# A set order of TensorE, VectorE and ScalarE while the weights of a matrix product come in

## The chip, the cores and the metric

One core of one Trainium2 chip runs the kernel. The metric is device time in microseconds (us), the median of several executions. The profile is of one execution, so its span (1517.6 us before) differs by a few us from the medians.

## The reference, cut to what matters

```python
B, S, D = 8, 2048, 2048            # x: B x S x D, w: D x D, float32
cs = np.cumsum(x, axis=1)
diff = cs - np.concatenate([zeros, cs[:, :-1, :]], axis=1)   # x again
return np.matmul(diff, w).astype(np.float32)
```

The running sum and its difference cancel, so the work is x @ w: 128 row tiles of x (128 x 2048 each) times a 2048 x 2048 matrix.

## The kernel before: the parts that matter

In the long run the kernel scales w to 16 bit (one scale for all of w) and multiplies tiles of x in groups of four with a Strassen-like scheme, which needs sums and differences of blocks of w. It cannot begin that before all of w has come in, because the scale needs the maximum of all of w. So while w arrives (32 pieces of 512 KB), TensorE multiplies the first three row tiles plainly in bf16, with each piece cast by ScalarE and its absolute maximum taken by VectorE. The x of these three tiles is cast, turned on TensorE (a transpose into PSUM) and copied out. A fourth tile ("late") is turned the same way and multiplied with the scaled w. The program is written in a framework that orders instructions by itself where nothing is said; `tc.issue_after` fixes an order.

```python
def turn(t, xf, i):
    v = bank(6 + i % 2).bitcast(bf16)[:, :NB]
    xb = ring.tile([P, NB], bf16, name="xb", bufs=3)
    nc.vector.tensor_copy(xb, xf)                       # cast of x
    for kk in range(KQ):
        at = ds(kk * P, P)
        nc.tensor.transpose(v[:, at], xb[:, at], eye)
    ...  # copy v to t, on ScalarE or VectorE by turns

def taken(h, ko):                                       # one piece of w
    ...
    nc.scalar.copy(b, wt)                               # cast to bf16
    nc.vector.tensor_reduce(wmax[:, i : i + 1], wt, AX.X, MAX, apply_absolute_value=True)

for h in range(2):                                      # left, right half of w
    for ko in range(KO - KQ):
        if h == 0 and ko == KQ:
            for q in range(1, 4):
                load_x(q)
        fetch(h, ko)
        if h == 0 and ko == 0:
            turn_x(0)
        if h == 0 and KQ <= ko < KQ + 3:
            turn_x(ko - KQ + 1)
        taken(h, ko)
        for r in range(EARLY):
            plain(h, r, ko)                             # two products
    ...  # the last four pieces; for h == 1 the late tile's turns and the maximum of all
    for r in range(EARLY):
        for ko in range(KO - KQ, KO):
            plain(h, r, ko)
        plain_out(h, r)                                 # PSUM to SBUF, ScalarE or VectorE
```

Then come three tiles of the first group. Each is loaded, measured, narrowed to 16 bit, and transposed by DMA.

```python
def prepare(t, waste, xf=None):
    ...  # load of x on SyncE's queue
    m, _ = measure(xf, waste)      # ScalarE; writes a result nobody reads into "waste"
    s, _ = invert(m)
    xh, _ = narrow(xf, s)
    xT = place(t)
    turn_over(xT, xh)              # DMA transposition, on SyncE's queue
    return m, xT

got[PLAIN] = prepare(PLAIN, waste)
...  # scaling of w, 32 instructions on VectorE and ScalarE
got[PLAIN + 1] = prepare(PLAIN + 1, waste, ...)
got[PLAIN + 2] = prepare(PLAIN + 2, waste)
...
put(c, rows, ds(h * NH + n * NB, NB))      # the late tile's stores, GpSimd
...
fetch_x(PLAIN + 3)                         # loads of the next tiles, SyncE
fetch_x(PLAIN + 4)
```

## Time and profile before

| | before |
|---|---|
| median of the three runs that the prediction knew (with the fourth: 1520.87) | 1521.25 us (1518.13 to 1521.31) |
| profiled span | 1517.6 us |
| TensorE busy in the profile | 98% |
| VectorE, ScalarE busy | 73%, 57% |
| 6840 products at 0.2159 us | 1476.8 us |

A busy share averages over stages. A product's recorded duration (379 ns) overlaps the next one's, so "busy" hides slow spacing; count the products instead.

### The profile page before, as it was taken

Reading aid. Unit: us, or ns where it says so; the run is one execution under the profiler, and the core shown is the slowest. Engines: PE = TensorE matmul, PEld = TensorE weight load, DVE = VectorE, ACT = ScalarE, POOL = GpSimd, SP = SyncE. Lnnn points to the kernel's source line nnn. Section 1 sums busy time; section 2 is a strip of 40 time slices with the busy share of each in tenths; the row PEclk is TensorE's granted clock in tenths of the full one; section 3 lists DMA queues with packets and bytes.
Section 4 is the critical chain, followed back from the end, with each engine's and each line's share of the span. In section 5 each row is a group of like instructions: output and inputs, shape, how many; then the busy total and the mean of one; then the engine's idle time right before and its main releaser. Section 6 shows DMA issues by size and latency. Waiting matters only on the chain. (4 is left out here: it accounts for less than half of the span.)

```text
span 1517.6 us, 19099 instructions
## 1 busy us (share of the span) xinstructions
PE 1493.7 (98%) x6904; PEld 674.1 (44%) x6904; DVE 1105.5 (73%) x2067; ACT 861.9 (57%) x1102; POOL 9.8 (1%) x21
## 2 busy tenths in 40 slices
PE   7999999999999999999999999999999999999998
PEld 3344444444444444444444444444444444444443
DVE  7896876767776766776767776767776767777767
ACT  5866555656555656555665555565556565556551
POOL 0100000000000000000000000000000000000000
PEclk9999999999999999999999999999999999999999
DMA  9978788778878788788788788788877887887772
GB/s 363 359 192 222 226 246 218 237 219 240 221 240 219 232 225 247 217 243 223 221 236 239 218 240 230 214 223 247 232 236 208 231 230 233 241 233 222 220 207 111
DMA packets 321470, 351.49 MB, mean 232 GB/s; under 512 B 266848, under 2 KB 266848, under 8 KB 305376
## 3 DMA queue, kind: packets, MB, share of 16 engines
q1 hardware_dynamic: 319808, 345.56, 79.0%
q0 software_dynamic: 1280, 4.20, 0.8%
q8 instruction: 54, 0.88, 0.2%
q10 hardware_dynamic: 288, 0.52, 0.1%
q14 instruction: 40, 0.33, 0.1%
HBM read 150.99 MB, written 134.22 MB: 188 GB/s over the span
## 5 line engine op out<-in xcount | busy, mean ns | idle before, releaser
L414 DVE SCALAR_TENSOR_TENSOR c<-b,u,c 128x512 f32<-128x512 f32 (+1 forms) x883 | 674.9, 799 | 232.2 <-ACT c L409 110.3
L409 ACT ACTIVATE c<-b,u 128x512 f32<-128x512 f32 x496 | 315.1, 680 | 279.6 <-PE b L367 184.7
L367 PE MATMUL b<-W,xT 128*128 128x512 f16 x2048 | 462.5, 379 | 1.7 <-DVE c L414 1.1
L367 PE MATMUL b<-W,W 128*128 128x512 f16 x1764 | 412.1, 379 | 1.4 <-ACT c L409 1.4
L105 ACT ACTIVATE c<-fin 128x2048 f16<-128x2048 f32 x92 | 175.7, 1910 | 243.9 <-DMA out_dram<-c 216.6
L367 PEld LDWEIGHTS <-xT 128*128 128x128 f16 x2048 | 200.3, 98 | 243.9 <-issue 2.7
L367 PEld LDWEIGHTS <-W 128*128 128x128 f16 x2016 | 197.2, 98 | 239.8 <-issue 2.3
L116 ACT ACTIVATE fin<-fin,s 128x2048 f16<-128x2048 f32 x123 | 246.2, 2002 | 88.3 <-issue 45.2
L378 PEld LDWEIGHTS <-W 128*128 128x128 f16 x1560 | 152.2, 98 | 187.0 <-issue 2.4
L378 PE MATMUL b<-W,W 128*128 128x512 f16 x810 | 220.0, 379 | 0.8 <-DVE c L414 0.7
L378 PE MATMUL b<-W,xT 128*128 128x512 f16 x720 | 179.9, 379 | 0.0
L378 PE MATMUL b<-inner,W 128*128 128x512 f16 x660 | 176.4, 379 | 0.0
L378 PEld LDWEIGHTS <-xT 128*128 128x128 f16 x960 | 93.9, 98 | 113.3
L473 DVE TENSOR_REDUCE m<-m 128x1 f32<-128x4 f32 x29 | 4.6, 157 | 106.9 <-ACT b L465 106.9
L465 ACT ACTIVATE b<-fin 128x512 f32<-128x512 f32 x116 | 68.0, 586 | 13.7 <-DMA fin<-in_x_dram 13.4
L367 PE MATMUL b<-W 128*128 128x512 f16 x252 | 75.1, 379 | 0.1
L423 DVE TENSOR_TENSOR W<-W,xT 128x1024 f16<-128x1024 f16 x122 | 68.2, 559 | 3.2
L423 DVE TENSOR_TENSOR W<-xT,W 128x1024 f16<-128x1024 f16 x122 | 67.4, 552 | 0.0
L378 PE MATMUL b<-inner,xT 128*128 128x512 f16 x240 | 61.6, 379 | 0.0
L423 DVE TENSOR_TENSOR W<-xT,xT 128x1024 f16<-128x1024 f16 (+1 forms) x92 | 54.8, 596 | 1.1 <-DMA xT<-fin 1.1
L111 DVE TENSOR_SCALAR m<-m 128x1 f32<-128x1 f32 x124 | 18.5, 149 | 42.9 <-ACT c L105 41.6
L212 PE MATMUL b<-wb,xP 128*128 128x512 bf16 x192 | 46.5, 406 | 2.7 <-ACT wb L204 2.7
(56 smaller groups left out, 471.9 us busy)
## 6 DMA issues: line engine op xcount, KB each, us to landing
fin<-in_x_dram SPq DMA_DIRECT2D x124, 1024.0 KB, 5.5
out_dram<-c SPq DMA_DIRECT2D x247, 512.0 KB, 3.2
W<-in_w_dram SPq DMA_DIRECT2D x32, 512.0 KB, 10.2
W<-in_x_dram SPq DMA_DIRECT2D x12, 256.0 KB, 6.5
xT<-fin SPq DMA_TRANSPOSE x184, 5.0
out_dram<-o POOLq DMA_DIRECT2D x10, 256.0 KB, 5.2
out_dram<-wb POOLq DMA_DIRECT2D x6, 256.0 KB, 9.7
xP<-in_x_dram SPq DMA_DIRECT2D x1, 1024.0 KB, 7.4
```

Source lines behind the costliest of these rows:

```text
L105: return m, nc.scalar.activation(waste.bitcast(f16), xf, ABS, scale=1.0 / ROW, accum_out=m)
L111: nc.vector.tensor_scalar(m, m, TINY, None, MAX)
L116: return xh, nc.scalar.activation(xh, xf, COPY, scale=s)
L212: nc.tensor.matmul(ps[r][n], xP[:, r, ko, :], wb[h, ko][:, ds(n * NB, NB)], start=(ko == 0), stop=(ko == KO - 1),)
L367: nc.tensor.matmul(ps[n], a[k], b[k][:, n, :], start=(first and k == 0), stop=(k == KH - 1), skip_group_check=True,)
L378: nc.tensor.matmul(ps, a[k], b[k], start=(first and k == 0), stop=(k == 3), skip_group_check=True)
L409: after("act", lambda: nc.scalar.activation(c, p, COPY, scale=scale))
L414: "dve", lambda: nc.vector.scalar_tensor_tensor(c, p, scale, c, MUL, ADD)
L423: after("dve", lambda: nc.vector.tensor_tensor(dst.all, p.all, q.all, op))
L465: lambda: nc.scalar.activation(ps[i % 2], xf[:, at], ABS, scale=1.0 / ROW, accum_out=m4[:, i : i + 1],),
L473: after("dve", lambda: nc.vector.tensor_reduce(m, m4, AX.X, ADD))
```

## The change

Its intent is that TensorE always finds its next operand. All instructions of TensorE, VectorE and ScalarE in the w stage are chained in the order in which they are written; the x of the plain tiles is loaded a quarter at a time between pieces of w; its casts stand ahead of that step's maximum and its turns between the products of a step; three casts of the right half stand ahead of the left half's copies; the late tile's turns stand behind the last products. In the first group, the load of a tile goes behind two stores and the measurement's waste goes to another buffer.

```diff
-        def turn(t, xf, i):
+        def cast(xf):
+            xb = ring.tile([P, NB], bf16, name="xb", bufs=3)
+            after("dve", lambda: nc.vector.tensor_copy(xb, xf))
+            return xb
+
+        def turn(t, xb, i):
             v = bank(6 + i % 2).bitcast(bf16)[:, :NB]
-            xb = ring.tile([P, NB], bf16, name="xb", bufs=3)
-            nc.vector.tensor_copy(xb, xf)
             for kk in range(KQ):
                 at = ds(kk * P, P)
-                nc.tensor.transpose(v[:, at], xb[:, at], eye)
+                after("pe", lambda: nc.tensor.transpose(v[:, at], xb[:, at], eye))
 ...  (the same wrapping for the casts of w, maxima, products and copies out)
+        AHEAD = 3
+        LOOK = KQ - 1, KQ + 1, KQ + 3
 ...
+                if h == 0:
+                    if KQ - 1 <= ko < KQ + 2:
+                        load_x(ko - KQ + 2)
+                    fetch(h, ko)
+                    if ko == 0:
+                        for r in range(EARLY):
+                            turn_x(0, r, cast(resting(0, r)))
+                    if ko in LOOK:
+                        q = LOOK.index(ko) + 1
+                        xb = [cast(resting(q, r)) for r in range(EARLY)]
+                    taken(h, ko)
+                elif ko >= AHEAD:
+                    fetch(h, ko)
+                    taken(h, ko)
                 for r in range(EARLY):
                     plain(h, r, ko)
+                    if xb:
+                        turn_x(q, r, xb[r])
 ...
+            if h == 0:
+                for ko in range(AHEAD):
+                    fetch(1, ko)
+                for ko in range(AHEAD):
+                    taken(1, ko)
 ...  (first group)
         turn(g + 4)
-        fetch_x(g + 5)
 ...
         put(C12g, g, 1)
+        fetch_x(g + 5)
 ...
-        weigh(g + 5, b)
+        weigh(g + 5, c)
```

## The prediction

> **What bounds the kernel now.** I first read the busy time of each engine by stage, cutting the span where the timeline of TensorE changes character. Columns: stretch in us, its length, busy us (and instructions) of TensorE, of its weight loads, of VectorE (DVE), ScalarE (ACT) and GpSimd, the granted clock, the DMA share, GB/s.
>
> ```profile
> 0.00:23.00 23.00, 12.91 (x72) 6.58 (x73) 14.39 (x30) 9.80 (x13) 0.19 (x4) 0.94 0.91 334
> 23.00:41.40 18.40, 17.70 (x72) 7.50 (x72) 15.23 (x16) 12.59 (x15) 0.00 (x0) 0.89 1.03 409
> 41.40:63.00 21.60, 21.12 (x96) 9.27 (x95) 18.80 (x21) 16.59 (x21) 4.06 (x8) 1.00 0.91 362
> 63.00:84.40 21.40, 18.00 (x80) 7.18 (x81) 20.99 (x42) 21.40 (x22) 3.45 (x7) 1.00 0.97 291
> 84.40:134.00 49.60, 46.47 (x212) 20.59 (x211) 36.52 (x77) 25.49 (x29) 2.15 (x4) 1.00 0.71 190
> 134.00:400.00 266.00, 265.80 (x1232) 120.15 (x1230) 197.49 (x387) 152.26 (x200) 0.00 (x0) 1.00 0.84 232
> 400.00:800.00 400.00, 400.00 (x1853) 181.06 (x1852) 287.44 (x543) 229.58 (x299) 0.00 (x0) 1.00 0.81 229
> ```
>
> From 400 to 800 us, 1853 matmuls take 400 us: 0.2159 us each, no gap. From 134 us on TensorE is the whole bound (1232 x 0.2159 = 266.0 in 266.0). Before that, 256 products and 64 transposes take 84.4 us where 256 x 0.2159 = 55.3 would do, 29 us lost; 212 products take 49.6 instead of 45.8, 3.8 lost. The last 318 us lose 6.5 more (1443 x 0.2159 = 311.5) at the tail. The diff touches no part of the steady groups or the tail, so at most about 33 us are in play, and less because w has to arrive.
>
> Who sets the end of the first 84 us? I followed VectorE through it (start, us, engine, line, operation, count, [idle before <- releaser]).
>
> ```profile
> 22.25 14.73 DVE L206 TENSOR_REDUCE wmax<-W 128x1 f32<-128x1024 f32 x13
> 40.16 1.29 DVE L233 COPY o<-b 128x512 f32<-128x512 f32 x2 [3.17 <-PE b L212]
> 41.36 16.98 DVE L206 TENSOR_REDUCE wmax<-W 128x1 f32<-128x1024 f32 x15
> 58.38 0.19 DVE L263 TENSOR_REDUCE wred<-wmax 128x1 f32<-128x32 f32 x1
> ...
> 59.52 0.75 DVE L282 TENSOR_SCALAR W<-W,uinv 128x1024 f16<-128x1024 f32 x1
> 62.40 0.69 DVE L233 COPY wb<-b 128x512 f32<-128x512 f32 x1 [2.13 <-PE b L212]
> ```
>
> The maxima of w (1.13 us each, 32 of them) run back to back to 58.38, although DMA ran out of queued work at about 57.5 and the last w came some microseconds sooner (2 MB of x, 5 us at 410 GB/s, were queued behind it). Only after the last maximum does the scale exist, and only then can the 25 scalings of w on VectorE (0.67 each) and the seven on ScalarE (1.1 each) start. They end at 82.55 and 83.53; the late tile's 64 products trickle behind them and end at 84.57. So in this stretch the bound is VectorE's queue, then ScalarE's; TensorE, which has only 13.8 us of work after 63, is not. Any TensorE time saved ahead of 63 us counts only so far as it releases VectorE or ScalarE.
>
> The 3.8 us after 84.4 are plain waits in TensorE's timeline:
>
> ```profile
> 128.16 0.38 PE L367 MATMUL b<-W,W 128*128 128x512 f16 x1 [1.17 <-ACT c L409]
> ...
> 133.00 0.38 PE L367 MATMUL b<-W,xT 128*128 128x512 f16 x1 [0.87 <-DVE c L414]
> ```
>
> with 0.20 and 0.28 beside them and 0.56 at 102.43. ScalarE itself stood still for 4.30 us until 127.42 on a store (out_dram<-c), then 1.21 more on another store before it could measure a tile. In the DMA queue of SyncE, the load of x at 118.99 had waited for its buffer, and three stores whose data was older sat behind it, issued only from 119.37.
>
> ```profile
> 127.42 1.26 ACT L409 ACTIVATE c<-b,u 128x512 f32<-128x512 f32 x2 [4.30 <-DMA out_dram<-c]
> 129.89 1.91 ACT L105 ACTIVATE c<-fin 128x2048 f16<-128x2048 f32 x1 [1.21 <-DMA out_dram<-c]
> ...
> 118.99 0.34 SPq L99 DMA_DIRECT2D fin<-in_x_dram  x1
> 119.37 1.86 SPq L419 DMA_DIRECT2D out_dram<-c  x3
> ```
>
> **What the Trainium skill says.** "TensorE: Matmul & The Clock Gate", section "Architectural detail: the array is 16× 32×32, not 1× 128×128", says ScalarE and VectorE take their queues strictly in order and TensorE runs its matmuls in order. The trace agrees: VectorE idled 3.17 us ahead of two copies although more w was there for the maxima behind them. So where an instruction stands is what the change really changes. The same page, "What's actually happening", says the array falls to half clock when it has been idle: the granted clock was 0.50 from 22 to 26 us, after the transposes, and the products there were issued 0.43 us apart. "Perfetto Trace Analysis", section "Roofline", puts 16 DMA engines at about 435 GB/s for one core; 409 GB/s at a full DMA share from 23 to 41 us is near that, so w cannot come faster.
>
> **The change, part by part.** It adds and removes no data work: the built program has 13810 rows on TensorE in both. It moves instructions.
>
> 1. Turns of x between products (loads of x spread over w3 to w5, casts ahead of that step's maximum). Saved: TensorE's stretch from 16.36 to 23.07, 6.7 us of transposes alone, and the half clock after it (72 products in 17.70, 2.15 over 72 x 0.2159). Paid: each turn now waits for its own w block and comes between ScalarE's casts. I scheduled it by hand with the trace's arrivals (w3 at 14.5 instead of 12.2, w5 20.9, w7 23.5) and durations (cast of w 1.04, maximum 1.13, product 0.216, four transposes about 0.5 to their end, copy 0.4). TensorE begins the steps 3, 5, 7 and 8 at about 15.6, 22.0, 27.2 and 30.5. In the kernel before it has done 25 of its 72 products by 30.5 (10 at half clock, then full), thus also stands at step 8. So the left half ends at about 30.5 + 48 x 0.2159 = 40.9 against 40.8: no gain, the idle time is only cut into pieces.
>
> 2. VectorE in that stretch. Before, its idle time between 4.1 and 58.4 is 1.10 + 0.70 + 0.85 + 0.44 + 1.71 + 0.16 + 0.49 + 0.80 + 3.17 = 9.4 us. After, the 3.17 goes (row by row order of the last 24 products frees banks 3.5 us before the end, and two maxima are put ahead of the copies), but in the three turning steps the copies out of PSUM stand right behind a maximum and wait for a product and the transposes: 0.85 + 1.0, 1.6, 0.7 + 1.0 = 5.2 us in place of about 3.2. With waits for w0 to w3 (about 2 us) and the first two (1.8) I get 9 to 9.5 us. The last maximum therefore stands where it was, 58.4, give or take 1.5.
>
> 3. Three right-half casts ahead of the stores: TensorE's 1.03 us wait at 41.79 for a cast goes. But VectorE reaches its two copies with 11 maxima still to do from 29.95: 29.95 + 11 x 1.13 = 42.4, done 43.7, so the right half's first step may wait 2 us for these banks and TensorE may end at 63.9 instead of 62.9. Off the path, as shown above.
>
> 4. After the scale. In the built order three scalings now stand before VectorE's first copy instead of one, so they fill the 2.13 us it idled; ScalarE's first copies need only the first row's products (at about 60.4, not 61.9, since the order of the last 24 stays row by row). VectorE's last scaling: 59.6 + 25 x 0.67 + copies 1.3 + casts 1.45 + late copies 0.75 + small ones 0.9 = 80.7, plus about 0.6 of waiting, 81.3 against 82.55. ScalarE from 60.4 instead of 61.9 over 21.6 us of work ends at about 82.1 against 83.53. The late stage so ends at about 83.2 instead of 84.5: **1.3 us gained**.
>
> 5. First group: the load of x goes behind the stores of C22 and C12, and the measurement's waste goes to buffer c. The store of C22 can be issued at about 115.3, after the transposes in the queue, instead of 119.4, so ScalarE's copy no longer waits until 127.4 and the 1.37 us at 128 go; the measurement does not wait 1.21, and the 1.15 at 133 go with it. The load itself waited for its buffer until 118.99 anyway and loses little. **2.5 us gained.**
>
> Sum 3.8 us; 1521.25 - 3.8 = 1517.4, put at 1517.3.
>
> **Rivals.** (a) Interleaving really lifts the w stage: if VectorE's copies find the transposes ready, its idle falls from 9.4 to about 5 us and the scale comes 4 us earlier: 1513. For it: the intent, and 44 us of VectorE work in a 54 us stage. Against: its strict order behind w's arrivals. (b) The interleaved turns leave TensorE under-fed from 16 to 30 us (about 30 products and 36 transposes, some 60% busy), the clock falls to half for longer and drags the copies and the maxima: 2 to 4 us given back, 1519 to 1521. For it: the 0.50 at 22 to 26 us. (c) x of the first group arrives late because its load is now behind stores, so that the stall at 128 is merely replaced by one on the measurement: the 2.5 us vanish, 1520. Against: the load waited for a buffer, not for its place.
>
> **Range and chances.** The late end is uncertain by about 2.5 us, the stall by 1, and three runs of before alone spread 3 us. Together some 3 to 4 us either way, with rival (a) stretching the fast side: 1511.5 to 1521. Two per cent is 30 us, all that is lost before 134 us with w not yet there for most of it: faster 0.01, slower 0.005, the rest within.
>
> **What would show it.** Right: last maximum within 57 to 60 us, the scalings' end at 81 to 82.5 on both engines, first product of the group at 83 to 84, no wait over 0.3 us from 125 to 134, the stretch from 134 on unchanged. Wrong: the last maximum before 56 (rival a), a granted clock of 0.50 for over 6 us (b), a wait on a measurement near 128 (c), or any new wait in the steady groups.

## The result

The changed kernel took 1521.17 us (median of four runs, 1519.15 to 1522.44), the kernel before 1520.87 in the same rounds. A ratio here is the mean time of one kernel's runs over that of the other's of the same rounds, so it is not quite the ratio of the medians: 1.0005, 95% interval 0.9987 to 1.0022. No gain can be seen. The profiled execution of the changed kernel is the fastest of its four (1519.15).

The stages of the changed kernel, in the same cut and with the same columns as in the prediction:

```profile
0.00:23.00 23.00, 11.80 (x58) 5.46 (x59) 13.89 (x25) 9.21 (x10) 0.19 (x4) 1.00 0.90 327
...
41.40:63.00 21.60, 19.94 (x93) 8.88 (x92) 20.38 (x24) 16.16 (x19) 4.35 (x8) 1.00 0.92 367
63.00:84.40 21.40, 19.08 (x92) 8.03 (x91) 20.75 (x41) 21.34 (x23) 5.54 (x9) 1.00 0.95 283
84.40:134.00 49.60, 45.69 (x212) 20.39 (x210) 36.40 (x77) 24.44 (x26) 0.74 (x2) 1.00 0.78 199
```

The clock stays at 1.00 in every stage. But the stretch from 84.4 to 134 us has the same 212 products as before: whatever was gained in it was lost in it. VectorE's timeline, where the prediction saw the bound of the first 84 us (start, us, engine, line, operation, count, idle before and its releaser):

```profile
30.01 12.47 DVE L221 TENSOR_REDUCE wmax<-W 128x1 f32<-128x1024 f32 x11
42.40 1.27 DVE L252 COPY o<-b 128x512 f32<-128x512 f32 x2
43.60 14.72 DVE L221 TENSOR_REDUCE wmax<-W 128x1 f32<-128x1024 f32 x13
58.36 0.19 DVE L293 TENSOR_REDUCE wred<-wmax 128x1 f32<-128x32 f32 x1
...
59.50 2.08 DVE L317 TENSOR_SCALAR W<-W,uinv 128x1024 f16<-128x1024 f32 x3
62.13 1.34 DVE L252 COPY wb<-b 128x512 f32<-128x512 f32 x2 [0.56 <-PE b L230]
```

The maxima end at 58.36 against 58.38: the new order did not move them. After the scale, three scalings fill the time in which VectorE had idled. Now TensorE's own timeline after that; the first line is the kernel before, the fence after it the changed one.

```profile
84.41 14.01 PE L367 MATMUL b<-W,xT 128*128 128x512 f16 x64
```

```profile
82.94 7.09 PE L402 MATMUL b<-W,xT 128*128 128x512 f16 x32
93.32 7.08 PE L402 MATMUL b<-W,xT 128*128 128x512 f16 x32 [3.30 <-DMA xT<-fin]
...
128.80 1.46 PE L402 MATMUL b<-W,W 128*128 128x512 f16 x6
...
132.26 7.93 PE L402 MATMUL b<-W,xT 128*128 128x512 f16 x36
```

The group starts 1.47 us earlier. Then, after 32 of its first 64 products, TensorE waits 3.30 us for a transposed tile (xT<-fin); before, the 64 ran through. At 128 and 132 us the old waits are gone. Putting the start of the same product side by side in both timelines gives the account:

| product | before | changed | changed - before |
|---|---|---|---|
| first of the group | 84.41 | 82.94 | -1.47 |
| 33rd (before: 84.41 + 32 x 0.2159) | 91.32 | 93.32 | +2.00 |
| first after the wait on a copy near 103 | 102.43 | 104.42 | +1.99 |
| first at the old stall | 128.16 | 128.80 | +0.64 |
| first at the second old stall | 133.00 | 132.26 | -0.74 |
| after a wait near 157 in both | 157.11 | 157.05 | -0.06 |
| after the last wait | 1511.26 | 1511.17 | -0.09 |

So both forecast gains are there, and a wait of 3.3 us that nothing in the prediction named ate most of them. Another 0.68 us (from -0.74 to -0.06) went between 133 and 157 us: near 150 the changed kernel waits 0.44 + 0.20 us for a copy of ScalarE that the kernel before does not wait for, and at 157 it waits 0.36 instead of 0.20 us.

Why is the third tile late? The queues of SyncE and GpSimd, first the kernel before, then the changed one (the columns are those of the timeline; xT<-fin at 83.72 and 84.43 is the third tile's transposition, out_dram<-o are the late tile's four stores, 1 MB):

```profile
79.59 4.04 SPq L127 DMA_TRANSPOSE xT<-xP  x2
83.72 1.84 SPq L127 DMA_TRANSPOSE xT<-fin  x1
...
84.40 2.27 POOL L221 DMA_DIRECT2D out_dram<-o  x4 [16.93 <-ACT o L323]
```

```profile
78.53 0.34 SPq L99 DMA_DIRECT2D fin<-in_x_dram  x1
78.97 5.37 SPq L127 DMA_TRANSPOSE xT<-xP  x2
84.43 5.11 SPq L127 DMA_TRANSPOSE xT<-fin  x1
...
82.91 2.27 POOL L240 DMA_DIRECT2D out_dram<-o  x4 [15.79 <-ACT o L358]
```

Before, the transposition was issued 0.7 us ahead of the stores. Because the late stage ends earlier, the stores now start at 82.91, 1.5 us ahead of the transposition, which itself is 0.7 us later. The issuing alone takes 5.11 us instead of 1.84 (second column). The time from issue to landing is the last column of these lines, first before, then changed:

```profile
xT<-fin SPq DMA_TRANSPOSE x1, 6.4
```

```profile
xT<-fin SPq DMA_TRANSPOSE x1, 8.8
```

It lands at 84.43 + 8.8 = 93.2 instead of 90.1. TensorE would have wanted it at 82.94 + 6.9 = 89.8. The Trainium skill, "DMA: Bandwidth & Descriptors", section "Issuing engines are not separate DMA queues", says that transfers run on the same 16 DMA engines and interleave whoever issued them; this trace agrees: from 90 to 93 us GpSimd's queue moved 0.26 MB and SyncE's 0.28 MB. The stores were ahead most of the time: from 86 to 87 us they moved 0.39 MB and SyncE's queue next to nothing, where in the kernel before SyncE's queue moved 0.20 MB, all of it transposition. The next runs put a price on it.

### The profile page after: what moved, and what is told of

Read it like the earlier page. It is cut to its first block, busy times and chain, and to the rows that moved or that the text cites. A ratio compares the mean times of both kernels' runs of the same rounds, so it can differ in the third digit from the quotient of the medians.

```text
span 1517.4 us, 19101 instructions
## 1 busy us (share of the span) xinstructions
PE 1489.0 (98%) x6904; PEld 673.1 (44%) x6904; DVE 1105.2 (73%) x2067; ACT 862.8 (57%) x1102; POOL 10.8 (1%) x21
## 4 chain that ended last, share of the span: by engine, by line
PE 89%; DVE 1%; issue 0%; DVEq 0%; ACT 0%
PE b L402 53%; PE b L413 36%; DVE c L436 0%; DVE W L445 0%; DVEq L861 0%; ACT b L487 0%; DVE u L520 0%; DVE m L495 0%; DVE m L111 0%; DVE s L112 0%; DVEq L436 0%; DVE xT L445 0%
```

## The experiments

Five rounds each unless told otherwise. "Span" is the profiled span, to be set beside 1517.6 before and 1517.4 changed. It is one execution; the spans of the kernel before lie between 1516.3 and 1521.3. All results were correct. Four runs have the run "the load behind the third transposition" as their base and were made later, on other chips, without it: they are compared with it through the ratio to the kernel before, and through single profiles.

**Part 5 alone.** The kernel before with the moved load and the other waste buffer.

```diff
         turn(g + 4)
-        fetch_x(g + 5)
 ...
         put(C12g, g, 1)
+        fetch_x(g + 5)
 ...
-        weigh(g + 5, b)
+        weigh(g + 5, c)
```

> The kernel before with part 5 of the change alone (load of x behind the stores, waste into buffer c). Theory 1 (my part 5 was right): no wait over 0.3 us of TensorE from 125 to 134, 2.5 us less, profiled span 1515.1 against 1517.6, and no wait on a transposed tile near 91-93. Rival: TensorE, being earlier, meets a new wait further on (as the 0.64 us at 150 in the changed kernel), so that only about 1.7 us remain, span 1515.9.

Measured: 1518.43 us against 1519.68, ratio 0.9992 (0.9979 to 1.0004), span 1516.6. There is no wait from 125 to 134 us and none on a tile, but one of 0.44 + 0.20 us at 150. This profiled execution happened to have its last maximum 1.43 us later than before with the same program up to there, so the span understates it: from the product at 102.43 (here 103.87, 1.44 later) to the one at 1511.26 (here 1510.42, 0.84 earlier) it gains 2.28 us. The interval of the ratio contains 1, so the runs alone do not show this gain; the profile does. There theory 1 holds in the main, and the rival is right that a little is given back.

**The start alone.** The reverse of that edit, made in the changed kernel.

> The changed kernel with part 5 undone: only the order of the first 84 us is new. Theory 1: the first product of the group stays at 83 (1.5 us gained), the 3.3 us wait on the transposed tile stays, and the waits of 1.37 and 1.15 us near 130 are back, so it is slower than the kernel before by about 1.8 us, span 1519.4. Rival: as TensorE comes 2 us later there, the store has landed and those waits are gone without part 5: then like the changed kernel, span 1517.4.

Measured: 1522.18 against 1519.68, ratio 1.0018 (1.0006 to 1.0031), span 1518.4. The first product of the group is at 83.06, the wait on the tile is 2.31 us (forecast 3.3), and near 130 us the waits are 0.95 + 0.20 and 0.80 + 0.28, somewhat smaller than before (1.17, 0.20, 0.87, 0.28), because TensorE comes later. Theory 1 is right in kind, the rival accounts for 0.3 us. The new start by itself is slower than the old one.

**The stores behind the third transposition.** Only the four stores differ from the changed kernel: they come later, and from SyncE's queue instead of GpSimd's.

```diff
-        turn_over(xT, xh)
+        turned[0] = turn_over(xT, xh)
 ...
-                put(c, rows, ds(h * NH + n * NB, NB))
+                with tc.issue_after(turned[0].ins):
+                    nc.sync.dma_start(out2[rows, ds(h * NH + n * NB, NB)], c)
```

> The changed kernel, but the late tile's four stores (1 MB) stand in SyncE's queue behind the third tile's transposition instead of being issued by GpSimd at 82.9. Theory A (these stores, now 1.5 us earlier, get ahead of the transposition on the DMA engines): the third tile is there at about 90.5 instead of 93.2, TensorE's wait shrinks from 3.3 to under 1 us, 2.5 us less, span 1515. Theory B (the load of 1 MB of x that stands ahead of the second tile's transposition is the cause): the wait stays within 0.7 us of 3.3, span about 1517.4.

Measured: 1516.06 against 1519.68, ratio 0.9976 (0.9963 to 0.999), span 1514.7. SyncE's queue in this run:

```profile
79.77 5.20 SPq L127 DMA_TRANSPOSE xT<-xP  x2
85.06 1.83 SPq L127 DMA_TRANSPOSE xT<-fin  x1
86.94 3.28 SPq L361 DMA_DIRECT2D out_dram<-o  x4
```

The load of x still stands ahead and the second tile still takes 5.20 us to issue, as in the changed kernel. The third tile is issued even later (85.06), but lands 5.2 us after that, at 90.3, and TensorE does not wait at all. Theory A's forecast came true (span 1515) and B's did not (1517.4): with the load left in place, moving the stores alone is enough. This run does not separate their later time from the other queue; the next one leaves the stores as they are.

**The load behind the third transposition.** Again a change of SyncE's queue alone.

```diff
-        turn_over(xT, xh)
+        last["sp"] = turn_over(xT, xh)     # the later loads are chained behind it
```

> The changed kernel, but the load of x for the fourth tile stands behind the third tile's transposition in SyncE's queue instead of ahead of the second's. Theory B: the transpositions run from 78.1 at once, the third is there by 89, the wait of 3.3 us is gone, span 1514.2. Theory A: some gain too, because the transposition then comes before the stores at 82.9, but not more than 2.5 us. Rival C (neither: the transpositions are held up by what was queued before 78 us): the third tile comes at 92 or later, wait at least 2 us, and the load, being later, may cost another wait at 98.

Measured: 1516.14 against 1519.68, ratio 0.9977 (0.9965 to 0.999), span 1514.4.

```profile
78.36 2.62 SPq L127 DMA_TRANSPOSE xT<-xP  x2
81.29 1.96 SPq L127 DMA_TRANSPOSE xT<-fin  x1
83.31 2.64 SPq L99 DMA_DIRECT2D fin<-in_x_dram  x2
```

The third tile is issued at 81.29, ahead of the stores (83.17 here), and lands in 4.3 us. No wait on it, none at 98. Here theory B's forecast fits (span 1514.2), and the span is 3.0 us under the changed kernel's, more than theory A allowed (2.5). The DMA traffic from 81 to 82 us says why, first in the changed kernel, then in this run:

```profile
DMA packets 44, 0.36 MB, mean 360 GB/s; under 512 B 0, under 2 KB 0, under 8 KB 0
```

```profile
DMA packets 831, 0.21 MB, mean 213 GB/s; under 512 B 831, under 2 KB 831, under 8 KB 831
```

The transposition's packets are the small ones. In the changed kernel the second tile's transpositions have been issued by then (from 78.97), but the load's large packets run first, and the third tile comes after the second. So the wait needed both, the load ahead of the second tile and the stores ahead of the third: taking away either one removes it. The kernel before has the load in the same place (46 packets in that microsecond, none small) and does not wait; what the change added are the earlier stores. Rival C falls. In this run TensorE waits 0.89 + 0.20 us at 147.

**The old start with both.** Is the new order of the first 84 us worth anything once the transposition is on time?

```diff
 (on top of part 5 alone, in the kernel before)
-        turn_over(xT, xh)
+        turned[0] = turn_over(xT, xh)
 ...
-    last = {}
+    last = {"sp": turned[0]}
```

> The kernel before, with part 5 and with the load of x behind the third transposition: the order of the first 84 us is the old one. Theory (the new order is worth 1.5 us once the transposition is no longer late): first product of the group at about 84.4, no wait on a tile, 1.5 us slower than the same kernel with the new order, span about 1515.9. Rival: the transposition comes so early here too that the new order is worth nothing: span 1514.4.

Measured: 1517.07 against 1520.64, ratio 0.998 (0.9967 to 0.9992), span 1514.8. It was run at another time. The first product is at 84.15, without a wait on a tile. The theory held for the start (84.15 against 83.07) but not to the end: the wait at 147 is 0.23 + 0.20 us here against 0.89 + 0.20 with the new start, and the spans differ by 0.4 us. The two ratios, 0.998 and 0.9977, cannot be told apart. So the new order of the w stage is worth about a microsecond where it acts and next to nothing at the end.

**Turns in one block per step.** Base: the load behind the transposition.

```diff
-                    if KQ - 1 <= ko < KQ + 2:
-                        load_x(ko - KQ + 2)
+                    if ko == KQ:
+                        for q in range(1, 4):
+                            load_x(q)
 ...
-                    if ko in LOOK:
-                        q = LOOK.index(ko) + 1
-                        xb = [cast(resting(q, r)) for r in range(EARLY)]
+                    if KQ <= ko < KQ + 3:
+                        q = ko - KQ + 1
+                        for r in range(EARLY):
+                            turn_x(q, r, cast(resting(q, r)))
                     taken(h, ko)
 ...
-                    if xb:
-                        turn_x(q, r, xb[r])
```

> The changed kernel with the load behind the third transposition, and the turns of x in one block ahead of step 4's products again instead of between products. Theory (part 1 and 2 of the prediction: interleaving gains nothing): last maximum within 1 us of 58.5, first product of the group within 0.7 us of 83.1, span 1513.7 to 1515.1; the granted clock falls to half for some us near 22. Rival: interleaving carries the 1.5 us, then the first product is at 84.5 and the span 1515.9.

Measured: 1520.66 against 1520.64, ratio 1.0004 (0.9991 to 1.0018), span 1519.4. A miss. The last maximum is taken by 62.87 instead of 58.5, the first product of the group is at 88.62. The stretch from 22 to 30 us by engine (columns as before; the clock is the third figure from the end):

```profile
22.00:30.00 8.00, 5.48 (x25) 2.60 (x22) 2.23 (x5) 2.11 (x3) 0.00 (x0) 0.50 1.03 410
```

VectorE works 2.23 of 8 us: its timeline has waits of 3.72, 2.22 and 4.00 us for transposes, and TensorE waits 1.62 to 1.76 us for casts. The clock is at half from 21.4 to 38.5 us, 17 us instead of the 6.8 of the kernel before. How much of the loss is the strict order, how much the clock, and how much the loads of x, which this edit also puts back in one place, was not separated. This edit is not the old order, in which the turns of three steps ran ahead of all products and maxima without such chaining, and which had its last maximum at 58.12 in the run above. So interleaving gains nothing over the old free order, as predicted, but once the order is fixed it saves 4 to 5 us (ratios, spans) over turning in blocks. My expectation overlooked the second half of that.

**The last 24 products block by block.** Base as above.

```diff
-            for r in range(EARLY):
-                for ko in range(KO - KQ, KO):
-                    plain(h, r, ko)
-                plain_out(h, r)
+            for ko in range(KO - KQ, KO):
+                for r in range(EARLY):
+                    plain(h, r, ko)
+            for r in range(EARLY):
+                plain_out(h, r)
```

> The changed kernel with the load behind the third transposition, and the last 24 products of each half block by block, as they stood before, instead of row by row. Theory (part 4: ScalarE and VectorE come to the scalings sooner because the first row's banks are ready 3.5 us before the end): ScalarE's first copy after the casts slips from 60.5 to about 62.5 or later, first product of the group 1 to 2 us later than 83.1, span about 1515.9. Rival: the three scalings ahead of VectorE's copies carry the gain alone: first product at 83.1, span 1514.4.

Measured: 1517.17 against 1520.64, ratio 0.9985 (0.9972 to 0.9997), span 1515.1. ScalarE's first copy behind the casts of w, in this run:

```profile
62.98 1.07 ACT L250 COPY wb<-b 128x512 f32<-128x512 f32 x2 [2.35 <-PE b L230]
```

With row by row order, in the base:

```profile
60.47 1.07 ACT L250 COPY wb<-b 128x512 f32<-128x512 f32 x2 [4.26 <-PE b L230]
```

The kernel before is written row by row too, but nothing fixes that order: in its trace this copy waits until 61.90, 1 us before the last product ends. The maxima end at the same time in both runs (58.42), the first product comes at 84.65 instead of 83.07, behind ScalarE's last scaling (84.02 instead of 82.2). Three scalings stand ahead of VectorE's copies here as well, so the rival falls. So the row by row order carries the 1.5 us of the start; at the end of the program 0.7 us of it remain in the spans, since the wait at 147 is shorter here. The time is not apart from the base beyond the intervals.

**Half of each maximum.** Base as above. The scale is deliberately not the one of all of w, so this is no candidate, only a probe.

```diff
-                    wmax[:, i : i + 1], wt, AX.X, MAX, apply_absolute_value=True
+                    wmax[:, i : i + 1], wt[:, :NB], AX.X, MAX, apply_absolute_value=True
```

> The changed kernel with the load behind the third transposition, each maximum of w over the first 512 of its 1024 columns only (the scale is then not that of all of w, on purpose; the result should still be within tolerance). Theory (VectorE's queue bounds the w stage): last maximum at about 56, soon after the last w at 55, TensorE's 1.4 us wait at 43 gone, first product of the group at 80.5 to 81.5, span about 1512.5. Rival (w's arrival or TensorE bounds it): last maximum earlier, but first product within 0.7 us of 83.1, span 1514.4.

Measured: 1514.12 against 1520.64, ratio 0.9961 (0.9949 to 0.9974), span 1512.2. VectorE near the end of w:

```profile
55.25 0.69 DVE L221 TENSOR_REDUCE wmax<-W 128x1 f32<-128x512 f32 x1 [0.58 <-DMA W<-in_w_dram]
55.97 0.19 DVE L293 TENSOR_REDUCE wred<-wmax 128x1 f32<-128x32 f32 x1
```

Each maximum now waits for its piece of w, so arrival is the bound; the last comes 2.5 us earlier, the first product of the group at 81.13, and 2.2 us are kept to the end. So VectorE's queue was the bound of the w stage with the new order, as the prediction said. The kernel before was not probed; there the last 15 maxima stand as close (16.98 us without a wait).

**Another waste buffer in the second group.** The wait at 147 comes from ScalarE: with the load behind the transposition, its measurement at 138.66 had waited 1.47 us for a store out of buffer c. The edit is on that base.

```profile
138.66 1.91 ACT L105 ACTIVATE c<-fin 128x2048 f16<-128x2048 f32 x1 [1.47 <-DMA out_dram<-c]
```

```diff
-            weigh(h + 1, c)
+            weigh(h + 1, b)
```

> The changed kernel with the load behind the third transposition, and the measurement of the second group writing its waste into buffer b (its store is issued earlier) instead of c. Theory (the gain of the start is given back at 147 us, where a measurement waits 1.47 us for a store out of c): ScalarE's wait before that measurement and TensorE's 0.89 + 0.20 us near 147 are gone or under 0.3, about 0.8 us less, span 1513.6. Rival (the store out of b lands no sooner, or TensorE waits for ScalarE's queue anyway): span 1514.4.

Measured: 1515.41 against 1519.6, ratio 0.9971 (0.9959 to 0.9984), span 1513.1. The measurement in this run:

```profile
136.95 1.91 ACT L105 ACTIVATE c<-fin 128x2048 f16<-128x2048 f32 x1
```

It waits for nothing, and TensorE has no wait from 102 to 152 us. Theory shown. Last maximum and first product (82.79) were 0.3 us earlier in this execution by chance, so about 1 us of the 1.3 in the span belongs to the edit. This version beats the kernel before with an interval clear of 1, and its five runs (up to 1516.68) all lie below the five of the changed kernel (from 1517.84). Its ratio, 0.9971, and the base's, 0.9977, cannot be told apart.

**The changed kernel again**, on the same chip:

> The changed kernel again, on the same chip as the one above, for a comparison of the two. Span within 1 us of 1517.4, the wait on the third tile within 1 us of 3.3 us, time within 0.15% of the kernel before and 3 to 4 us above the other run of this call.

Measured: 1520.12 against 1519.6, ratio 1.0 (0.9986 to 1.0014), span 1519.1, wait on the tile 3.76 us. The span was 1.7 us longer than in its first profile, more than expected. 0.5 us of it is in that wait; and after it the granted clock was 0.50 from 93.3 to 96.7 us, so that the 32 products behind it took 8.46 us instead of 7.08. In the first profile, after 3.30 us, it had stayed at 1.00. The other run is 4.7 us faster (forecast 3 to 4).

## Why the prediction was wrong, by its own steps

- **Part 1, no gain from turns between products**: right. The steps began at 15.9, 22.5 and 30.6 us (steps 3, 5, 8; forecast 15.6, 22.0, 30.5), and the left half's 48 last products ran from 30.59, ending at 41.0 as forecast.
- **Part 2, the last maximum stays**: right, 58.36 against 58.38. The probe with half maxima shows that VectorE's queue set it with the new order.
- **Part 3, TensorE ends at 63.9, off the path**: right. It waited 1.44 + 0.22 us for VectorE's two copies at 43 us, and the late tile's turns began at 63.86.
- **Part 4, 1.3 us after the scale**: right. The scalings ended at 81.16 on VectorE and 82.04 on ScalarE (forecast 81.3, 82.1), and the first product came at 82.94, 1.47 us earlier. The run by blocks shows that the row by row order carries this.
- **Part 5, 2.5 us in the first group**: right in kind, slightly large. Between the products at 102 us and the end it was worth 2.28 us alone, because a measurement in the second group now met a store (1.02 us, ScalarE at 140.89) and gave some back; the edit of the waste buffer removes such a wait.
- **The sum, 3.8 us**: this is the step that failed. It let the 1.3 us pass on to the group as if the group's tiles were there. The third tile's transposition lands at 90.1 in the kernel before, while TensorE wanted it at 91.3: a slack of 1.2 us, less than the gain. Worse, the very gain of part 4 brought the late tile's stores ahead of that transposition, which the load of x already held back, so that it came at 93.2. The 3.3 us wait cost 3.47 us by the table above (from -1.47 to +2.00). Moving the stores, or moving the load, removes it and gives 0.9976 and 0.9977, some 3.6 us of 1520, close to the 3.8 I had predicted. That closeness is in part luck: the old start with both edits already gives 0.998, so the 1.3 us of part 4 hardly reach the end.
- **Rivals**: none of the three named this wait. Rival (a) falls, since the last maximum did not come earlier. Rival (c) looked for a late x in the first group, but at the wrong tile. Rival (b)'s clock did not fall in the changed kernel, yet it did in the run with turns in blocks.
- **The range**: 1521.17 lies just outside, above 1521.0. No sign in the last paragraph named the wait: "any new wait" was said of the steady groups, and this one is in the first group. The range had given it too little room. That the change stays within 2% was right.
- **A slip without effect**: the tail's loss is 317.6 - 311.5 = 6.1 us, not 6.5.

The second tile's two transpositions, too, are slow to issue behind the load: 5.2 to 5.5 us where the load was issued 0.44 us ahead of them, 3.84 and 4.04 where it was 1.3 to 1.4 us ahead, and 2.6 in the six runs with the load behind. This is the delay that left the third tile behind the stores. Why a transposition's issuing takes longer while other traffic runs, the traces do not show.

## What to carry to other kernels

When a stage is made to end sooner, ask what its end triggers, here four stores, and what those will then run ahead of. Before adding gains, write down for the next stage when each of its inputs lands and when it will now be wanted: a gain larger than the smallest slack is lost there. Here transfers that nobody waited for soon (outputs, a load for later) did less harm behind a transposition that TensorE was about to need.

## What the Trainium skill lacked or had wrong

- "DMA: Bandwidth & Descriptors", section "Issuing engines are not separate DMA queues": true here, but it gives no cost for a transposition that other traffic gets ahead of. One tile's transposition (128 x 2048, 16 bit) took 4.3 to 6.4 us from issue to landing where it was issued ahead of 1 MB of stores, and 7.8, 8.8 and 9.5 us in the three runs where it was issued behind them; its issuing alone took 1.7 to 2.0 and 5.1 to 5.6 us. TensorE's wait for it was 2.3 to 3.8 us in these three.
- "TensorE: Matmul & The Clock Gate", section "What's actually happening", lets the clock fall after at least one idle window of about 3.4 us; the page has no figure for how little work counts as idle. In the kernel before the clock was at 0.50 from 20.3 us on, although the longest idle gap of TensorE in its timeline from 16 to 23 us is 1.19 us: its records, almost all transposes, fill 2.50 of the 4.3 us from 16.2 to 20.5. The changed kernel, with transposes and products in 3.00 of the 6 us from 18 to 24 and 4.01 of those from 24 to 30, kept 1.00. So the busy share alone does not tell the two apart, and no threshold comes out of these traces.
